# Second feed-forward of a hybrid block: where the pair stage keeps its activation sums and weight differences, and when the last adaLN rows are computed

## The chip, the cores and the metric

The kernel runs on one core of one Trainium2 chip. The metric is the device time of one execution in microseconds (us), the median of several runs. The engines are TensorE (PE, matmuls), VectorE (DVE), ScalarE (ACT), GpSimd (POOL) and SyncE (SP), whose queue issues nearly all DMAs here. Each engine works through its own instructions in a fixed order.

## The reference

One block with 256 rows of 2048 values, all in float32. A vector c gives, by a 2048 x 18432 matrix (adaLN), nine vectors of 2048: a shift, a scale and a gate for each of three parts. The parts are a feed-forward, a mixer (differential attention beside a convolution), and a second feed-forward:

```python
def swiglu(h, w_gu, w_down):
    gu = jnp.einsum('bsd,df->bsf', h, w_gu)
    g, u = jnp.split(gu, 2, axis=-1)
    return jnp.einsum('bsf,fd->bsd', jax.nn.silu(g) * u, w_down)
...
    h = modulate(rms_norm(x, ffn2_norm[l]), sh2, sc2)
    x = x + FFN_RESIDUAL_WEIGHT * g2[:, None, :] * swiglu(h, ffn2_w_gu[l], ffn2_w_down[l])
```

Here w_gu is 2048 x 11264 and w_down 5632 x 2048. The change touches the second feed-forward alone.

## The kernel before

**Products.** A float32 operand is split into two parts: hi, rounded to the fp32r type by a cast on ACT, and lo, the rest, by a subtraction on DVE. A product is three matmuls (mm3, L342, L346, L347): hi by hi, hi by the weight's lo, and lo by the weight's hi. A weight tile is 128 x 2048 values (1 MB), loaded into one of four raw buffers (L307) and split in two halves of 1024 columns (L318 on ACT, L320 on DVE) into four whi and four wlo buffers. A tile gives 24 matmuls of 512 columns: four row blocks by two row tiles (t) by three.

**adaLN.** The matrix is laid out as 144 rows of 128 x 2048 (ada, L195 and L196): each is loaded into a raw buffer too, and multiplied and summed with c, broadcast in the buffer c_bc, in one DVE instruction. Rows 96 to 127 are the scales and shifts of the second feed-forward, rows 128 to 143 its gates. ada_share(r, limit) adds r rows to a credit for each weight tile and computes a row when the credit reaches one; ada_until(j) computes all rows up to j at once.

**The second feed-forward** (ffn with base 96). Gate and up columns are taken in 22 chunks of 512 (256 of each). Chunks 0 to 13 go in the usual way: four weight tiles each, of which the first (k blocks 0 to 3) is done early, and its result kept in parts[c]. The norm comes in four pieces of 512 columns by two row tiles (Norm.piece): a DMA transposes it (turn), and complete scales and splits it; after_tiles(n, ...) puts a step off by n weight tiles. Chunks 14 to 21 go as four **pairs**: the two chunks' first tiles (b11, b21 in one raw buffer, b12, b22 in the other) are taken together in seven products in place of eight (pair_first, Winograd's form of Strassen), each of six matmuls. For that, pair_sums makes four sums of activations once for all pairs, and each pair makes four differences of weights. Six ordinary weight tiles complete a pair. Chunk 13 comes last, and then the product with w_down (down_strassen).

In pair_first the products stand in this order: b11 (into c22), b12 - b11 (c12), t2 = b22 - b12 (c22), b21 - t2 (c21), b21 (c11), t2 - b11 (c22), b22 (c12). Between them kept() copies c22 or c12 into a tmp buffer (L719), since c22 and c12 add up over several products.

finish(c, ...) turns a chunk's result into operands of w_down: it adds the kept part (L935), applies silu (L936) and the product (L937), a DMA transposes it, and a cast and a subtraction split it (L364, L365) into a block that lives until the end. It is called during the following chunk or pair.

**Buffers and order.** General blocks (blk, 28 of 4 KB a partition) hold the norm's operands (8), parts, finished chunks and whatever is in hand; tmp has 6 buffers. A scheduler sets each engine's order at build time, and a buffer goes to the next that asks when it comes free. Before, the sums of the pairs are put into c_bc (L680), so that all adaLN rows have to be done first: ada_until(144) stands ahead of pair_sums (L994).

## Time and profile before

| | |
|---|---|
| median of 3 runs | 1827.68 us (1826.13 to 1827.97) |
| the profiled execution | 1827.56 us, its span 1824.5 us |
| granted TensorE clock, mean | 0.995 |
| busy in the span | PE 98%, DVE 85%, ACT 58%; SP's DMA queue 75.7% of the 16 DMA engines' time |
| matmuls | 8009 |
| second feed-forward's pairs | four, from 1398.8 us to about 1568 us |

Times in the trace are counted from the start of the span. A matmul's duration (about 390 ns) overlaps with the next one's; what counts is the distance between starts. In the rows of a timeline stand the start, the duration, the engine, the line, the operation and the tiles; "x2" merges two in a row, and brackets give the idle time before and what ended it. A row by stretch has its bounds, its length, the busy time and (x) the instructions of PE, PEld (weight loads), DVE, ACT and POOL, then the granted clock, the share of the DMA engines and GB/s.

### The profile page before, as it was taken

Reading aid. Unit: us, or ns where it says so; the run is one execution under the profiler, and the core shown is the slowest. Engines: PE = TensorE matmul, PEld = TensorE weight load, DVE = VectorE, ACT = ScalarE, POOL = GpSimd, SP = SyncE. Lnnn points to the kernel's source line nnn. Section 1 sums busy time; section 2 is a strip of 40 time slices with the busy share of each in tenths; the row PEclk is TensorE's granted clock in tenths of the full one; section 3 lists DMA queues with packets and bytes.
Section 4 is the critical chain, followed back from the end, with each engine's and each line's share of the span. In section 5 each row is a group of like instructions: output and inputs, shape, how many; then the busy total and the mean of one; then the engine's idle time right before and its main releaser. Section 6 shows DMA issues by size and latency. Waiting matters only on the chain.

```text
span 1824.5 us, 21716 instructions
## 1 busy us (share of the span) xinstructions
PE 1790.1 (98%) x8009; PEld 1471.6 (81%) x8009; DVE 1551.4 (85%) x2000; ACT 1063.1 (58%) x1577; POOL 29.2 (2%) x29
## 2 busy tenths in 40 slices
PE   7999999999999999999999999999998999999998
PEld 5778888888888888888888888878887888878887
DVE  7889889898898778898999798797988777699877
ACT  7554455565454434567798647656665666555453
POOL 0000000000000000000110000000000000000000
PEclk8999999999999999999999999999999999999999
DMA  9979999898999888765444497898996666655552
GB/s 378 360 306 315 351 340 318 321 340 330 341 351 357 323 345 325 288 252 193 177 149 162 164 361 289 322 343 287 341 346 236 206 220 237 218 190 213 202 216 106
DMA packets 118138, 507.17 MB, mean 278 GB/s; under 512 B 53601, under 2 KB 54033, under 8 KB 60561
## 3 DMA queue, kind: packets, MB, share of 16 engines
q1 hardware_dynamic: 118032, 505.81, 75.7%
q8 instruction: 62, 1.02, 0.2%
q14 instruction: 44, 0.35, 0.1%
HBM read 492.37 MB, written 2.12 MB: 271 GB/s over the span
## 4 chain that ended last, share of the span: by engine, by line
PE 87%; DVE 8%; ACT 2%; issue 2%; DMA 1%; POOLq 0%; POOL 0%; DVEq 0%; SPq 0%; ACTq 0%
PE acc L346 27%; PE acc L347 27%; PE acc L342 26%; DVE wlo L320 2%; PE tp L342 2%; PE tp L347 2%; PE tp L346 2%; DVE raw L196 1%; DMA xall<-in_x_dram 1%; PE acc L1269 1%; ACT whi L318 1%; DVE blk L1161 1%; DVE wlo L551 0%; DVE blk L320 0%; ACT whi L550 0%
## 5 line engine op out<-in xcount | busy, mean ns | idle before, releaser
L346 PE MATMUL acc<-wlo,blk 128*128 128x512 f32 x2248 | 878.8, 391 | 10.0 <-DVE wlo L320 9.9
L342 PE MATMUL acc<-whi,blk 128*128 128x512 f32 x2251 | 873.6, 392 | 7.1 <-ACT whi L318 5.5
L347 PE MATMUL acc<-whi,blk 128*128 128x512 f32 x2248 | 877.0, 390 | 0.1
L318 ACT CAST whi<-raw 128x1024 fp32r<-128x1024 f32 x565 | 578.9, 1044 | 393.3 <-PE acc L347 246.2
L320 DVE TENSOR_TENSOR wlo<-raw,whi 128x1024 fp32r<-128x1024 f32 x565 | 669.4, 1209 | 152.2 <-ACT whi L318 151.1
L346 PEld LDWEIGHTS acc<-wlo,blk 128*128 128x128 f32 x2248 | 422.8, 188 | 105.0 <-DVE wlo L320 16.5
L342 PEld LDWEIGHTS acc<-whi,blk 128*128 128x128 f32 x2251 | 423.3, 188 | 96.0 <-ACT whi L318 6.8
L347 PEld LDWEIGHTS acc<-whi,blk 128*128 128x128 f32 x2248 | 422.7, 188 | 88.4 <-DVE blk L419 0.8
L196 DVE CUSTOM_DVE_ANT_0 raw<-raw,c_bc 128x2048 f32<-128x2048 f32 x142 | 323.9, 2283 | 1.1 <-DMA raw<-in_w_ada_dram 1.0
L550 ACT CAST whi<-raw 128x1024 fp32r<-128x1024 f32 (+1 forms) x56 | 52.9, 946 | 69.0 <-PE tp L347 31.9
L551 DVE TENSOR_TENSOR wlo<-raw,whi 128x1024 fp32r<-128x1024 f32 (+1 forms) x56 | 60.8, 1087 | 20.2 <-ACT whi L550 20.0
L936 ACT ACTIVATE blk<-blk 128x256 f32<-128x256 f32 x88 | 35.3, 416 | 64.1 <-DVE blk L935 63.9
L1161 DVE SCALAR_TENSOR_TENSOR blk<-blk,cst,blk 128x247 f32<-128x247 f32 (+21 forms) x176 | 70.3, 457 | 0.0
L770 ACT COPY blk<-acc 128x512 f32<-128x512 f32 x56 | 32.5, 589 | 44.0 <-PE acc L347 42.2
L935 DVE TENSOR_TENSOR blk<-acc,blk 128x512 f32<-128x512 f32 x72 | 47.2, 683 | 10.8 <-PE acc L347 10.8
L956 ACT COPY blk<-blk 128x1024 uint16<-128x1024 uint16 x33 | 44.2, 1355 | 9.6 <-DMA blk<-blk 9.5
L342 PE MATMUL tp<-whi,blk 128*128 128x512 f32 x127 | 49.4, 389 | 0.0
L346 PE MATMUL tp<-wlo,blk 128*128 128x512 f32 x127 | 49.4, 389 | 0.0
L347 PE MATMUL tp<-whi,blk 128*128 128x512 f32 x127 | 49.4, 389 | 0.0
L342 PE MATMUL acc<-blk,blk 128*128 128x512 f32 x104 | 40.7, 394 | 0.5 <-ACT blk L334 0.5
L346 PE MATMUL acc<-blk,blk 128*128 128x512 f32 x100 | 39.1, 391 | 0.5 <-DVE blk L320 0.5
L940 ACT COPY blk<-tmp 128x1024 uint16<-128x1024 uint16 x33 | 34.2, 1048 | 9.0 <-DVE tmp L937 8.7
(264 smaller groups left out, 1246.9 us busy)
## 6 DMA issues: line engine op xcount, KB each, us to landing
raw<-in_w_gu_dram SPq DMA_DIRECT2D x161, 1024.0 KB, 6.7
raw<-in_w_ada_dram SPq DMA_DIRECT2D x142, 1024.0 KB, 6.3
raw<-in_w_dn_dram SPq DMA_DIRECT2D x88, 1024.0 KB, 5.1
raw<-in_w_in_dram SPq DMA_DIRECT2D x40, 1024.0 KB, 4.8
raw<-in_w_out_dram SPq DMA_DIRECT2D x16, 1024.0 KB, 4.8
raw<-in_w_gu_dram SPq DMA_DIRECT2D x8, 768.0 KB, 5.7
blk<-in_w_gu_dram SPq DMA_DIRECT2D x10, 512.0 KB, 13.5
blk<-gate_line SPq DMA_DIRECT2D x6, 512.0 KB, 5.7
```

The source lines that it names most:

```text
L196: nc.vector.tensor_tensor_reduce(out=raw, in0=raw, in1=c_bc, scale=1.0, scalar=0.0, op0=ALU.mult, op1=ALU.add, accum_out=ada_cols[g][:, j ...
L318: nc.scalar.copy(out=hi[:, :m, :], in_=rw)
L320: nc.vector.tensor_sub(out=lo[:, :m, :], in0=rw, in1=hi[:, :m, :].bitcast(F32))
L342: nc.tensor.matmul(acc, ah, wh, start=start, stop=False, skip_group_check=more)
L346: nc.tensor.matmul(acc, ah, wl, start=False, stop=False, skip_group_check=more)
L347: return nc.tensor.matmul(acc, al, wh, start=False, stop=stop, skip_group_check=more)
L550: nc.scalar.copy(out=hi[:, :n, :], in_=src)
L551: nc.vector.tensor_sub(out=lo[:, :n, :], in0=src, in1=hi[:, :n, :].bitcast(F32))
L935: nc.vector.tensor_add(out=p[:, t, :], in0=accs[t], in1=us[t] if us else p[:, t, :])
L936: nc.scalar.activation(out=p[:, t, :256], in_=p[:, t, :256], func=AF.Silu)
L956: nc.scalar.copy(out=src.bitcast(U16).rearrange("p i t (s b) -> p b t i s", b=2), in_=turned.rearrange("p (b t i s) -> p b t i s", b=2, t= ...
L1161: nc.vector.scalar_tensor_tensor(out=y[:, d:], in0=u, scalar=w, in1=y[:, d:], op0=ALU.mult, op1=ALU.add)
```

## The change

Five things change, all in the second feed-forward:

- pair_sums puts its sums into two general blocks, which are in hand until the last pair's products; c_bc stays as it is until down_strassen.
- pair_first has no block t2. The differences are made in place, one after the other in b12 and b11, each as soon as the product of the one before is split.
- ada_until(144) goes. The rows go on in the pairs: credit for two tiles behind pair_first, and for one behind each of the six tiles.
- The rate of the rows in the single chunks and the pairs is 0.4 a tile in place of 0.72.
- In Norm.piece the steps of the second row tile of pieces 1 and 2 are put off by one weight tile more (behind = 2 + t).

```diff
-            behind = 1 if self.base == 0 or kb == 3 else 2
+            behind = 1 if self.base == 0 or kb == 3 else 2 + t
...
-        keep = cbp.tile([P, 2, 2, 4, P], F32R, tag="c_bc", name="sums")
+        keep_hi, keep_lo = blk([P, 2, 4, P], F32R), blk([P, 2, 4, P], F32R)
...
-            hi, lo = keep[:, 0, j], keep[:, 1, j]
+            hi, lo = keep_hi[:, j], keep_lo[:, j]
...
-        t2 = blk([P, 2, 512])
+        w11 = split(b11)
         nc.vector.tensor_sub(out=b12, in0=b12, in1=b11)
-        nc.vector.tensor_sub(out=t2, in0=b22, in1=b12)
-        times(c22, lambda j: act(j, 0), split(b11), True)
+        times(c22, lambda j: act(j, 0), w11, True)
         u11 = kept(c22)
-        nc.vector.tensor_sub(out=b11, in0=t2, in1=b11)
         times(c12, lambda j: sums[j][0], split(b12), True)
         u22 = kept(c12)
-        times(c22, lambda j: sums[j][1], split(t2))
+        nc.vector.tensor_sub(out=b12, in0=b22, in1=b12)
+        times(c22, lambda j: sums[j][1], split(b12))
         u12 = kept(c22)
-        nc.vector.tensor_sub(out=t2, in0=b21, in1=t2)
-        times(c21, lambda j: act(2 + j, 1), split(t2), True)
+        nc.vector.tensor_sub(out=b11, in0=b12, in1=b11)
+        nc.vector.tensor_sub(out=b12, in0=b21, in1=b12)
+        times(c21, lambda j: act(2 + j, 1), split(b12), True)
...
-                ada_until(144)
                 sums = pair_sums(st)
...
                 us = pair_first(w_gu, c, act, sums, banks)
+                ada_share(2 * ada_b[0], ada_b[1])
...
                         mm_tile(banks[2 * n:2 * n + 2], w, act, 4 * pc, False, pc == 3, more=True)
+                        ada_share(*ada_b)
...
-    ffn(norm2, w_gu2, w_dn2, 128, (0.72, 128), (0.72, 144), None, [], [[c] for c in range(3, 10)], [])
+    ffn(norm2, w_gu2, w_dn2, 128, (0.72, 128), (0.4, 144), None, [], [[c] for c in range(3, 10)], [])
```

The new lines of pair_first stand in the changed kernel at L728 (b22 - b12), L731 (into b11) and L732 (b21 - b12); L723 is the first difference in both.

First place, DVE, the last steps of the sums before the pairs. L196 is an adaLN row (its second entry reads the sum out), L683 to L689 form the sums, L692 splits them, L935 and L937 belong to the chunk before. Before:

```order
L196 ISA raw_11290,ada_10985<-raw_11290,c_bc 128x2048
L196 ISA ada_10985 128x1
L687 TENSOR_TENSOR tmp_11309<-tmp_11309,tmp_11307 128x128
L935 TENSOR_TENSOR blk_9647<-acc_11162,blk_9647 128x512
L196 ISA raw_11293,ada_10985<-raw_11293,c_bc 128x2048
L196 ISA ada_10985 128x1
L689 TENSOR_TENSOR tmp_11309<-tmp_11307,tmp_11309 128x128
L201 TENSOR_TENSOR ada_10985<-ada_10985,cst 128x8
L937 TENSOR_TENSOR tmp_11356<-blk_9647 128x256
L935 TENSOR_TENSOR blk_9647<-acc_11163,blk_9647 128x512
L692 TENSOR_TENSOR sums<-tmp_11300,sums 128x512
L692 TENSOR_TENSOR sums<-tmp_11309,sums 128x512
```

And now, from the first step of the sums on:

```order
L683 TENSOR_TENSOR tmp_11282<-blk_9035,blk_9036 128x512
L689 TENSOR_TENSOR tmp_11275<-tmp_11273,tmp_11275 128x128
L686 TENSOR_TENSOR tmp_11284<-tmp_11282 128x128
L688 TENSOR_TENSOR tmp_11284<-tmp_11282 128x128
L687 TENSOR_TENSOR tmp_11284<-tmp_11284,tmp_11282 128x128
L320 TENSOR_TENSOR wlo_11297<-raw_11293,whi_11295 128x1024
L692 TENSOR_TENSOR blk_11272<-tmp_11275,blk_11271 128x512
L689 TENSOR_TENSOR tmp_11284<-tmp_11282,tmp_11284 128x128
L365 TENSOR_TENSOR blk_11328<-blk_9605,blk_11328 128x512
L196 ISA raw_11374,ada_11373<-raw_11374,c_bc 128x2048
L196 ISA ada_11373 128x1
L692 TENSOR_TENSOR blk_11272<-tmp_11284,blk_11271 128x512
```

Two of the last three rows stand above among the steps of the second sum, the third just ahead of them; now the steps follow each other, with one row ahead of the last split.

Second place, DVE in the second pair, up to the low half of the fourth operand. L710 is the low half of an operand of the pair, named by what it is split from; L935 belongs to the pair before. Before:

```order
L724 TENSOR_TENSOR blk_11753<-raw_11751 128x1024
L320 TENSOR_TENSOR wlo_11719<-raw_11711,whi_11717 128x1024
L710 TENSOR_TENSOR wlo_11757<-raw_11749,whi_11756 128x1024
L935 TENSOR_TENSOR blk_11836<-acc_11433,tmp_11454 128x512
L727 TENSOR_TENSOR raw_11749<-blk_11753,raw_11749 128x1024
L710 TENSOR_TENSOR wlo_11770<-raw_11751,whi_11769 128x1024
L935 TENSOR_TENSOR blk_11836<-acc_11434,tmp_11512 128x512
L710 TENSOR_TENSOR wlo_11782<-blk_11753,whi_11781 128x1024
L935 TENSOR_TENSOR blk_11845<-acc_11435,tmp_11479 128x512
L732 TENSOR_TENSOR blk_11753<-raw_11749,blk_11753 128x1024
L935 TENSOR_TENSOR blk_11845<-acc_11436,tmp_11467 128x512
L710 TENSOR_TENSOR wlo_11795<-blk_11753,whi_11794 128x1024
```

And now:

```order
L935 TENSOR_TENSOR blk_11825<-acc_11412,tmp_11431 128x512
L710 TENSOR_TENSOR wlo_11754<-raw_11738,whi_11753 128x1024
L196 ISA raw_11822,ada_11373<-raw_11822,c_bc 128x2048
L196 ISA ada_11373 128x1
L728 TENSOR_TENSOR raw_11738<-raw_11738 128x1024
L935 TENSOR_TENSOR blk_11825<-acc_11413,tmp_11490 128x512
L731 TENSOR_TENSOR raw_11736<-raw_11738,raw_11736 128x1024
L710 TENSOR_TENSOR wlo_11767<-raw_11738,whi_11766 128x1024
L935 TENSOR_TENSOR blk_11834<-acc_11414,tmp_11456 128x512
L732 TENSOR_TENSOR raw_11738<-raw_11736,raw_11738 128x1024
L935 TENSOR_TENSOR blk_11834<-acc_11415,tmp_11443 128x512
L710 TENSOR_TENSOR wlo_11781<-raw_11738,whi_11780 128x1024
```

L724, which makes the third operand in a block of its own ahead of all splits, is gone; L728 makes it behind the low half of the second operand, and an adaLN row stands between the two.

ACT in the same pair: L709 is the cast of an operand, L719 the copy of a product. Before, from the third operand on:

```order
L709 CAST whi_11781<-blk_11753 128x1024
L936 ACTIVATE blk_11836<-blk_11836 128x256
L936 ACTIVATE blk_11845<-blk_11845 128x256
L719 COPY tmp_11766<-tp_11748 128x512
L709 CAST whi_11794<-blk_11753 128x1024
L719 COPY tmp_11779<-tp_11747 128x512
L709 CAST whi_11804<-raw_11749 128x1024
L719 COPY tmp_11791<-tp_11748 128x512
L709 CAST whi_11814<-raw_11749 128x1024
```

And now:

```order
L709 CAST whi_11766<-raw_11738 128x1024
L936 ACTIVATE blk_11825<-blk_11825 128x256
L719 COPY tmp_11751<-tp_11735 128x512
L719 COPY tmp_11763<-tp_11734 128x512
L936 ACTIVATE blk_11834<-blk_11834 128x256
L719 COPY tmp_11776<-tp_11735 128x512
L709 CAST whi_11780<-raw_11738 128x1024
L709 CAST whi_11790<-raw_11736 128x1024
L709 CAST whi_11800<-raw_11736 128x1024
```

The cast of the fourth operand stood behind the first copy, and stands now behind the third.

Third place, ACT in the fourth pair, from the fifth operand on; L318 casts the tile behind the pair, L364 splits finished chunks. Before:

```order
L709 CAST whi_12450<-raw_12395 128x1024
L719 COPY tmp_12425<-tp_12393 128x512
L709 CAST whi_12460<-raw_12395 128x1024
L719 COPY tmp_12437<-tp_12394 128x512
L709 CAST whi_12472<-raw_12397 128x1024
L936 ACTIVATE blk_12491<-blk_12491 128x256
L318 CAST whi_12502<-raw_12500 128x1024
L936 ACTIVATE blk_12491<-blk_12491 128x256
L318 CAST whi_12506<-raw_12500 128x1024
L719 COPY tmp_12470<-tp_12394 128x512
```

And now:

```order
L709 CAST whi_12447<-raw_12393 128x1024
L709 CAST whi_12457<-raw_12393 128x1024
L709 CAST whi_12469<-raw_12395 128x1024
L318 CAST whi_12499<-raw_12497 128x1024
L364 CAST blk_12280<-blk_12157 128x512
L364 CAST blk_12284<-blk_12166 128x512
L318 CAST whi_12503<-raw_12497 128x1024
L318 CAST whi_12533<-raw_12531 128x1024
L719 COPY tmp_12433<-tp_12392 128x512
```

The third copy (tmp_12437, now tmp_12433) stood behind the cast of the sixth operand, and stands now behind three casts of later tiles and two splits of chunks of the second pair.

## The prediction

> **What bounds the kernel now.** I read the page first, then the waits of TensorE (PE), then busy time by stretch, then the timeline at the one place that stands out.
>
> ```profile
> PE 1790.1 (98%) x8009; PEld 1471.6 (81%) x8009; DVE 1551.4 (85%) x2000; ACT 1063.1 (58%) x1577; POOL 29.2 (2%) x29
> PE acc L342 <- ACT whi L318: 4.6, 1, 4.6
> 1350.00:1400.00 50.00, 45.02 (x184) 35.90 (x183) 43.88 (x56) 25.43 (x30) 0.00 (x0) 0.93 0.81 294
> 1400.00:1450.00 50.00, 50.00 (x220) 40.61 (x219) 38.22 (x38) 32.84 (x41) 0.00 (x0) 1.00 0.54 176
> 1450.00:1500.00 50.00, 50.00 (x221) 41.02 (x220) 38.98 (x42) 34.16 (x41) 0.00 (x0) 1.00 0.68 223
> 1500.00:1550.00 50.00, 50.00 (x221) 41.12 (x220) 37.09 (x38) 33.55 (x41) 0.00 (x0) 1.00 0.69 248
> ```
>
> PE is busy 98% of the span, and the change neither adds nor takes a matmul: it can only remove or add PE waits. The second row is the longest wait behind the first 15 us, 4.6 us. It lies in the stretch 1350 to 1400 (184 matmuls where the next stretches have 220 and 221, granted clock 0.93), just before the four pairs. The pairs themselves (1400 to 1550) run without a wait, with 11 to 13 us of every 50 free on VectorE (DVE).
>
> ```profile
> 1373.78 0.39 PE L346 MATMUL acc<-wlo,blk 128*128 128x512 f32 x1
> 1374.00 0.39 PE L347 MATMUL acc<-whi,blk 128*128 128x512 f32 x1
> 1379.04 1.22 PE L342 MATMUL acc<-whi,blk 128*128 128x512 f32 x2 [4.64 <-ACT whi L318]
> ...
> 1385.33 0.52 PE L346 MATMUL acc<-wlo,blk 128*128 128x512 f32 x1
> 1385.69 0.40 PE L347 MATMUL acc<-whi,blk 128*128 128x512 f32 x1
> 1382.00:1384.00 2.00, 2.00 (x6) 1.57 (x5) 2.00 (x2) 1.08 (x2) 0.00 (x0) 0.50 0.24 98
> 1386.00:1388.00 2.00, 2.00 (x11) 1.64 (x10) 1.23 (x1) 0.24 (x1) 0.00 (x0) 1.00 0.73 303
> ```
>
> Matmuls follow each other by 0.227 us at full clock. From 1374.00 to 1385.69 only 15 start, worth 3.4 us, so this place costs 11.7 - 3.4 = **8.3 us**: 4.6 of waiting, and the rest because the clock then stands at 0.50 until 1385.5.
>
> **The change, part by part.** *The gap goes.* The cast PE waits for stands on ScalarE (ACT) behind the casts of the sums (L691), and those wait for a DVE chain between whose steps three adaLN rows stand (the order of before, in the section on the change). With the rows spread, the sums' steps stand in the changed order together, about three tiles ahead of the first pair. DVE does then, in the last 16.3 us before the pairs, six halves of weights (6.8), the sums (about 4), one row (2.2) and some 2.5 of other steps: 15.5 of 16.3, and it runs four halves (10.9 us) ahead. I see no new wait there: -8.3.
>
> *Norm pieces.* Behind = 2 + t delays only the completion of the second row tile of pieces 1 and 2 by one weight tile.
>
> ```profile
> 1193.39 2.28 DVE L196 CUSTOM_DVE_ANT_0 raw<-raw,c_bc 128x2048 f32<-128x2048 f32 x1
> ...
> 1196.34 1.37 DVE L890 TENSOR_TENSOR blk<-acc,blk 128x512 f32<-128x512 f32 x2
> 1197.63 2.35 DVE L320 TENSOR_TENSOR wlo<-raw,whi 128x1024 fp32r<-128x1024 f32 x2
> 1198.89 0.50 PE L346 MATMUL acc<-wlo,blk 128*128 128x512 f32 x1 [1.46 <-DVE wlo L320]
> 1197.00:1199.00 2.00, 0.54 (x3) 0.12 (x2) 2.00 (x4) 1.97 (x4) 0.00 (x0) 1.00 0.83 348
> ```
>
> PE waits here 1.46 us for the half that DVE splits at 1197.63, behind two L890 steps. In the changed order one of the two stands behind that half, so it starts some 0.7 earlier: -0.8 (between 0 and the whole 1.5).
>
> *The differences in place, and the rows beside them.* I call the seven products of a pair p1 to p7, their split operands #1 to #7, and the start of p1 zero. A product is six matmuls, 1.36 us. The second pair of before:
>
> ```profile
> L342 PE MATMUL tp<-whi,sums x16: 389/389/497, 1442.7 to 1535.3; 128*128 128x512 f32 x16
> 1436.10 1.05 ACT L709 CAST whi<-raw 128x1024 fp32r<-128x1024 f32 x1 [1.71 <-PE acc L347]
> 1442.86 0.59 ACT L719 COPY tmp<-tp 128x512 f32<-128x512 f32 x1 [0.67 <-PE tp L347]
> 1443.34 1.05 ACT L709 CAST whi<-blk 128x1024 fp32r<-128x1024 f32 x1
> 1444.42 1.23 DVE L710 TENSOR_TENSOR wlo<-blk,whi 128x1024 fp32r<-128x1024 f32 x1 [0.95 <-ACT whi L709]
> 1478.02 0.68 DVE L935 TENSOR_TENSOR blk<-acc,tmp 128x512 f32<-128x512 f32 x1
> 1478.62 1.22 DVE L727 TENSOR_TENSOR raw<-blk,raw 128x1024 f32<-128x1024 f32 x1
> 1479.75 1.22 DVE L710 TENSOR_TENSOR wlo<-raw,whi 128x1024 fp32r<-128x1024 f32 x1
> 1371.56 2.28 DVE L196 CUSTOM_DVE_ANT_0 raw<-raw,c_bc 128x2048 f32<-128x2048 f32 x1
> 1373.77 0.08 DVE L196 DVE_READ_ACCUMULATOR2_ANT ada<- 128x1 f32 x1
> ```
>
> p2 starts at 1442.7, so zero is 1442.7 - 1.36 = 1441.3. The cast of #4 starts at 1443.34, behind the copy of p1 (L719), and its low half is ready at 1444.42 + 1.23 = 1445.65, that is 4.3; p4 starts at 3 x 1.36 = 4.1 and uses the low half in its second matmul, at 4.3. So #4 comes just in time: **whatever delays it, PE pays in full.** On DVE a step of 1024 costs 1.13 from start to start (1478.62 to 1479.75), L935 0.60, an adaLN row 2.21.
>
> Before, #3 is computed (L724) ahead of the pair into its own block. Now it overwrites b12, so it has to follow the split of #2, whose cast waits until PE frees a buffer: it ends at 1437.15, that is -4.2. From there the changed order on DVE gives: low half of #2 to -3.0, adaLN row to -0.8, L728 to 0.3, L935 to 0.9, L731 to 2.1, low half of #3 to 3.2, L935 to 3.8, L732 to 5.0. p3's second matmul, due at 2.95, starts at 3.2, and p3 ends at 4.4. ACT now copies p3 ahead of the cast of #4: copy to 5.1, cast to 6.2, low half to 7.4. p4's second matmul starts at 7.4 instead of 4.3: **+3.1**. The later operands follow by 1.13 each, faster than a product, and add nothing.
>
> The same steps for the other pairs. First: the row stands ahead of #2 (row to -3.7, #2 to -2.5, L365, L728, L731, #3 to 1.6, L935, L732 to 3.4), the copy of p3 behind the cast; low half of #4 at 5.8: +1.5. Third: as the second, with two small steps more: +3.4. Fourth: no row, and the same walk brings #4 at 4.4, so in place costs nothing by itself.
>
> But the fourth pair has another wait. The sums hold two of 28 blocks, where before one (t2) was taken and given back in each pair. With 8 blocks of activations, 13 finished chunks, one part, two chunks of the first pair, two sums and two of the second in hand, all 28 are taken; the second pair's chunks can't be split (L364, L365) until p5 frees the first activations. Behind that stand the sums of the third pair (L935), and behind those the copy of p3, which lacks a tmp buffer.
>
> ```profile
> 1417.51 0.62 ACT L364 CAST blk<-blk 128x512 fp32r<-128x512 f32 x1
> 1418.17 0.69 DVE L365 TENSOR_TENSOR blk<-blk,blk 128x512 fp32r<-128x512 f32 x1 [1.56 <-ACT blk L364]
> 1406.26 2.00 ACT L318 CAST whi<-raw 128x1024 fp32r<-128x1024 f32 x2
> ```
>
> p5 ends at 7.1. ACT does two L364 (to 8.7), two casts L318, the second only when p7 has freed its buffer (9.6 to 10.7), and then the copy (11.3). DVE does #7 (8.2), two L365 (9.5) and the four L935 (12.0), the first of which frees the tmp buffer in time; then the low half of the first tile behind the pair (13.1). So p6 starts at 11.3, and that tile goes on at 13.2, with the 47th matmul since zero, due at 46 x 0.227 = 10.4: **+2.8**. It is 0.5 if the blocks come free in time (what #7 costs alone), and 4 if each step slips by a few tenths.
>
> *The queue of SyncE.* Seven rows' loads move among the weights and take one of four raw buffers each.
>
> ```profile
> raw<-in_w_gu_dram SPq DMA_DIRECT2D x161, 1024.0 KB, 6.7
> raw<-in_w_ada_dram SPq DMA_DIRECT2D x142, 1024.0 KB, 6.3
> ```
>
> The second weight of a pair (b12, b22) now goes out when the row ahead of it is done on DVE, about -14.3; with 6.7 to land it is there at -7.6, L723 is done at -6.4, #1 at -5.3, and #2 isn't late. The row inside the pair goes out at -13.2, needed at -3.0: covered by 4. Were the cover gone, DVE would stand in order behind the row, a microsecond for a microsecond.
>
> The sum, against the profiled execution (1827.56, span 1824.5, 0.12 below the median of the runs): -8.3 - 0.8 + 1.5 + 3.1 + 3.4 + 2.8 = +1.7, that is **1829.3 us**.
>
> **The rivals.** *The clock falls again (slower).* In pairs 2 and 3 PE waits 1.8 us, starts one matmul, and waits 1.0 more. At 1.46 us the clock stayed at 1.00 (the row of 1197), at 4.64 it fell; nothing between is shown. If one matmul doesn't count, the two waits are one of 2.8. A fall costs 8.3 - 4.6 - 0.2 (a second wait there) = 3.4: two make 1836. It decides if the clock looks at a share of busy time. The Trainium skill (TensorE: Matmul & The Clock Gate, Why this matters for your kernels) asks for no idle gaps over about 3 us between bursts. By that, these waits leave the clock alone and the sum stays 1829.3; the two rows of this trace agree with it.
>
> *The rows find room (faster).* If a row's step comes earlier than the buffer for #2, it costs nothing: DVE has 11 to 13 us free in 50, and the walk takes every step in order at its latest. If the waits of the pairs come to 3 in place of 10.8: 1821.5. Against it: pairs of before are just in time with no row.
>
> *Rows land late (slower).* If three of the seven rows come 1.5 us late: 1833.8. For it: loads of 1024 KB take 6.3 to 6.7. Against it: the cover above.
>
> *The gap stays.* If it was made by late weights and not by the rows, 8.3 come back: 1837.6. Against it: the wait names a cast, and ACT had the sums' casts ahead of it.
>
> **How the numbers follow.** This kernel's measurement tells about 0.2% (3.7 us) from no change. Forecast, 1829.3 (its own range 1826.5 to 1831.2, the pairs' waits 8 to 12.7): 0.52, and it is within 0.2%. Rows find room, 1821.5: 0.17, faster. Clock 0.16, late rows 0.10, gap stays 0.05: slower, 0.31 together. The range runs from 1821.5 to 1836.0; it leaves out half of the faster case and, above, the last one and some of the clock's.
>
> **What would show it.** Right: no 4.6 us wait before the pairs and a clock of 1.00 there; PE waits of 2 to 3 us in each of pairs 2 and 3, before p4, put down to ACT L709 or DVE L710; one of about 2 us in pair 4, before p6, put down to the copy of p3. A clock under 1.00 between the pairs speaks for the first rival, PE without waits there for the second, DVE waits for a load of w_ada in the pairs for the third. Pairs' waits under 5 or over 14 us in all make the forecast wrong.

## The result, and the profile after

The changed kernel takes 1836.3 us, the median of six runs (1833.5 to 1843.2), against 1827.8 before (1826.1 to 1828.4): a ratio of 1.0052, 95% interval 1.0035 to 1.0070. That is 8.5 us slower, where the prediction had 1829.3 and a range that ended at 1836.0. The profiled execution is the fastest of the six: 1833.5 us, span 1831.4, that is 6.9 longer than before.

The gap before the pairs is gone, as forecast. By stretch, the same 12 us of the kernel before and of the changed one:

```profile
1374.00:1386.00 12.00, 7.13 (x18) 4.88 (x17) 10.24 (x16) 7.41 (x10) 0.00 (x0) 0.72 0.84 265
```

```profile
1374.00:1386.00 12.00, 12.00 (x54) 9.95 (x53) 11.02 (x16) 5.90 (x7) 0.00 (x0) 1.00 0.87 289
```

PE runs 54 matmuls there in place of 18, at a clock of 1.00. But the pairs, which had no wait at all before, now have these, the four longest entries of PE's waits from 1390 to 1550 (the total in us, how often, the longest):

```profile
PE acc L342 <- ACT whi L709: 5.5, 5, 1.6
PE acc L346 <- DVE wlo L710: 1.8, 3, 0.8
PE tp L342 <- ACT whi L318: 1.1, 1, 1.1
PE tp L342 <- ACT tmp L719: 0.7, 1, 0.7
```

The second pair on PE, with the names p1 to p7 and #1 to #7 of the prediction, from p3's first matmul to p4's first; the last row is p5's first matmul, which now runs ahead of p4's second:

```profile
1439.20 0.39 PE L342 MATMUL tp<-whi,blk 128*128 128x512 f32 x1
1439.87 0.50 PE L346 MATMUL tp<-wlo,blk 128*128 128x512 f32 x1 [0.28 <-DVE wlo L710]
...
1440.90 0.40 PE L347 MATMUL tp<-whi,blk 128*128 128x512 f32 x1
1442.92 0.51 PE L342 MATMUL acc<-whi,blk 128*128 128x512 f32 x1 [1.62 <-ACT whi L709]
1443.87 0.50 PE L342 MATMUL acc<-whi,blk 128*128 128x512 f32 x1 [0.44 <-ACT whi L709]
```

Matmuls follow by 0.227 when nothing is late. Whatever two starts are further apart than that is lost: here 0.44 at p3's second matmul, 1.79 ahead of p4 (1442.92 - 1440.90 - 0.23), 0.72 behind p4's first: 2.95. The cause stands on DVE as the prediction walked it:

```profile
1432.37 1.23 DVE L710 TENSOR_TENSOR wlo<-raw,whi 128x1024 fp32r<-128x1024 f32 x1 [0.94 <-ACT whi L709]
1433.51 2.29 DVE L196 CUSTOM_DVE_ANT_0 raw<-raw,c_bc 128x2048 f32<-128x2048 f32 x1
1435.72 0.08 DVE L196 DVE_READ_ACCUMULATOR2_ANT ada<- 128x1 f32 x1
1435.72 1.22 DVE L728 TENSOR_TENSOR raw<-raw 128x1024 f32<-128x1024 f32 x1
...
1440.33 1.22 DVE L732 TENSOR_TENSOR raw<-raw,raw 128x1024 f32<-128x1024 f32 x1
1441.46 0.69 DVE L935 TENSOR_TENSOR blk<-acc,tmp 128x512 f32<-128x512 f32 x1
1442.90 1.22 DVE L710 TENSOR_TENSOR wlo<-raw,whi 128x1024 fp32r<-128x1024 f32 x1 [0.75 <-ACT whi L709]
```

The low half of #2, the adaLN row, L728, then the chain to L732, and the low half of #4 at 1442.90: DVE waits for nothing from 1432.37 on but once, for the cast of #4.

Summed in this way over every place, in us, each from the one profiled execution of the kernel; the median beside it is that of all its executions. A star is one window of half clock (3.41 us, worth about 1.7; the section on the hardware), included in the number:

| kernel | ahead of the pairs, 1255 to 1386 | pair 1 | pair 2 | pair 3 | pair 4 | median | ratio to before, 95% interval |
|---|---|---|---|---|---|---|---|
| before | 8.6 ** | 0.2 | 0.1 | 0.2 | 0.1 | 1827.8 | |
| changed, profiled | 0.8 | 3.7 | 3.2 | 5.6 * | 3.3 | 1836.3 | 1.0035 to 1.0070 |
| 1: rate 0.82 alone | 6.2 | 0.3 | 0.1 | 0.2 | 0.1 | 1825.5 | 0.9982 to 0.9999 |
| 2: and in place | 5.6 | 4.2 * | 0.8 | 0.8 | 0.8 | 1829.6 | 1.0007 to 1.0025 |
| 3: sums in blocks, not in place | 0.6 | 8.7 ** | 0.2 | 0.1 | 0.6 | 1829.3 | 1.0005 to 1.0023 |
| 4: both, rows ahead | 0.8 | 9.7 ** | 0.8 | 0.8 | 3.3 | 1835.4 | 1.0031 to 1.0058 |
| 5: rows late in the pairs | 0.2 | 6.8 ** | 5.4 * | 5.7 * | 3.4 | 1840.0 | 1.0059 to 1.0086 |
| 6: changed, again | 3.9 * | 3.3 | 4.8 * | 5.6 * | 3.3 | 1837.5 | 1.0046 to 1.0071 |
| 7: norm pieces alone | 9.2 ** | 0.2 | 0.2 | 0.1 | 0.1 | 1826.8 | 0.9992 to 1.0009 |
| 8: two rows earlier | 4.5 | 0.2 | 0.1 | 0.2 | 0.1 | 1823.6 | 0.9974 to 0.9992 |
| 9: other differences in place | 6.1 | 1.6 | 3.7 * | 2.1 | 2.1 | 1831.9 | 1.0017 to 1.0037 |
| 10: cast ahead of copy | 0.3 | 6.0 * | 4.8 * | 6.1 * | 3.4 | 1838.4 | 1.0040 to 1.0065 |
| 11: three rows earlier, 0.66 | 5.2 | 0.2 | 0.2 | 0.2 | 0.1 | 1824.0 | 0.9979 to 0.9996 |
| 12: no row in pair 1 | 0.0 | 5.6 * | 6.0 * | 2.7 | 3.4 | 1837.5 | 1.0051 to 1.0078 |
| 13: copy behind the cast in pair 1 | 0.0 | 5.9 ** | 3.2 | 5.6 * | 3.3 | 1835.8 | 1.0032 to 1.0062 |
| 14: both of these | 1.9 | 2.0 | 6.3 ** | 2.7 | 3.4 | 1833.9 | 1.0025 to 1.0053 |

Changed against before, in the two profiles: -7.8 ahead of the pairs, and +3.5, +3.1, +5.4 and +3.2 in the pairs, +7.4 together, for 6.9 more of span; most of the rest was gained in the first 40 us, where the two kernels are alike.

### The profile page after: what moved, and what is told of

It reads as the page before. It is cut to its first block, busy times and chain, and to the rows that moved or that the text cites. A ratio compares the mean times of both kernels' runs of the same rounds, so it can differ in the third digit from the quotient of the medians.

```text
span 1831.4 us, 21722 instructions
## 1 busy us (share of the span) xinstructions
PE 1791.6 (98%) x8009; PEld 1470.7 (80%) x8009; DVE 1552.3 (85%) x2000; ACT 1065.6 (58%) x1577; POOL 29.2 (2%) x29
## 5 line engine op out<-in xcount | busy, mean ns | idle before, releaser
L318 ACT CAST whi<-raw 128x1024 fp32r<-128x1024 f32 x565 | 579.3, 1044 | 397.7 <-PE acc L347 241.1
L320 DVE TENSOR_TENSOR wlo<-raw,whi 128x1024 fp32r<-128x1024 f32 x565 | 670.0, 1211 | 150.6 <-ACT whi L318 149.2
L196 DVE CUSTOM_DVE_ANT_0 raw<-raw,c_bc 128x2048 f32<-128x2048 f32 x142 | 324.1, 2285 | 4.1 <-DMA raw<-in_w_ada_dram 4.1
L342 PE MATMUL tp<-whi,blk 128*128 128x512 f32 x143 | 56.0, 391 | 1.8 <-ACT whi L318 1.1
L956 ACT COPY blk<-blk 128x1024 uint16<-128x1024 uint16 x33 | 44.4, 1355 | 21.3 <-DMA blk<-blk 21.3
L346 PE MATMUL tp<-wlo,blk 128*128 128x512 f32 x143 | 55.9, 391 | 0.3 <-DVE wlo L710 0.3
L347 PE MATMUL tp<-whi,blk 128*128 128x512 f32 x143 | 55.7, 389 | 0.0
L935 DVE TENSOR_TENSOR blk<-acc,blk 128x512 f32<-128x512 f32 x72 | 47.1, 684 | 9.9 <-PE acc L347 9.9
L709 ACT CAST whi<-raw 128x1024 fp32r<-128x1024 f32 x28 | 28.4, 1050 | 26.4 <-PE acc L347 10.0
L710 DVE TENSOR_TENSOR wlo<-raw,whi 128x1024 fp32r<-128x1024 f32 x28 | 33.4, 1222 | 10.9 <-ACT whi L709 10.8
L342 PE MATMUL acc<-blk,blk 128*128 128x512 f32 x104 | 40.7, 394 | 0.7 <-ACT blk L334 0.7
```

The source lines that it names most:

```text
L196: nc.vector.tensor_tensor_reduce(out=raw, in0=raw, in1=c_bc, scale=1.0, scalar=0.0, op0=ALU.mult, op1=ALU.add, accum_out=ada_cols[g][:, j ...
L318: nc.scalar.copy(out=hi[:, :m, :], in_=rw)
L320: nc.vector.tensor_sub(out=lo[:, :m, :], in0=rw, in1=hi[:, :m, :].bitcast(F32))
L342: nc.tensor.matmul(acc, ah, wh, start=start, stop=False, skip_group_check=more)
L346: nc.tensor.matmul(acc, ah, wl, start=False, stop=False, skip_group_check=more)
L347: return nc.tensor.matmul(acc, al, wh, start=False, stop=stop, skip_group_check=more)
```

## The experiments

Each kernel is the kernel before or the changed one with the edit shown. Losses are those of the table.

**1. The burst of rows alone.** The kernel before, rate 0.82.

```diff
-    ffn(norm2, w_gu2, w_dn2, 128, (0.72, 128), (0.72, 144), None, [], ...)
+    ffn(norm2, w_gu2, w_dn2, 128, (0.72, 128), (0.82, 144), None, [], ...)
```

> Of the change nothing is kept but the idea that no burst of adaLN rows stands ahead of the sums: the kernel before with the rate of the rows at 0.82 a tile in place of 0.72, so that all 16 are done when the sums are made (sums in c_bc, third difference in its own block, no row in the pairs). Theory (the burst of rows among the sums' steps made the gap of 8.3 us before the pairs, and nothing else in the change gains): about 1819.5, no wait before the pairs, pairs without a wait as before. Rival (the gap comes from late weights or from the sums themselves): it stays, about 1827.8.

Measured 1825.5, 1.4 faster than the runs of before beside it. The wait of 4.6 and the fall of the clock are gone, so the burst did make the gap. But the faster rate brought waits of its own, 6.2 us of them. PE's waits from 1326 to 1356 and, in the second fence, from 1356 to 1381:

```profile
1332.38 0.50 PE L346 MATMUL acc<-wlo,blk 128*128 128x512 f32 x1 [1.46 <-DVE wlo L320]
1355.35 0.50 PE L346 MATMUL acc<-wlo,blk 128*128 128x512 f32 x1 [0.53 <-DVE wlo L320]
```

```profile
1362.54 0.50 PE L346 MATMUL acc<-wlo,blk 128*128 128x512 f32 x1 [1.46 <-DVE wlo L320]
1380.48 0.50 PE L346 MATMUL acc<-wlo,blk 128*128 128x512 f32 x1 [0.97 <-DVE wlo L320]
```

**2. And the differences in place.** As 1, with the pair_first of the changed kernel (L720 to L733), sums in c_bc.

> The first experiment's kernel (rate 0.82, sums in c_bc) with the differences made in place. No adaLN row stands in a pair. Theory (the in-place chain alone is just in time, as the walk gives low half #4 at 4.3 without the row, and it is the row of 2.2 us inside it that PE pays for): PE waits of at most 0.5 us a pair, about 1819.5 to 1821. Rival (the chain in place is itself too long, row or no row): some 3 us in each of pairs 1 to 3, about 1828.5.

Measured 1829.6: 4.1 more than the first. Both were partly wrong. Pairs 2 to 4 lose 0.8 each with no row inside, neither nothing nor 3: of the 3.2 and the 3.9 (without half clock) that pairs 2 and 3 lose in the changed kernel, the chain in place is 0.8. Pair 1 loses 2.5 besides half clock, with no row near: there the low half of #2 starts 3.3 us ahead of p1, in pair 2 4.1, and two short steps more (L365 and an L935) stand between it and the last difference.

**3. The sums in blocks, differences not in place.**

```diff
     (of the changed kernel:)
-    (0.4, 144)
+    (0.72, 144)
...
+        t2 = cbp.tile([P, 2, 512], F32, tag="c_bc", name=nm("t2"))
         nc.vector.tensor_sub(out=b12, in0=b12, in1=b11)
+        nc.vector.tensor_sub(out=t2, in0=b22, in1=b12)
     (and on as in the kernel before)
```

> The sums in two general blocks, as in the changed kernel, but the third difference in a place of its own as in the kernel before (it takes c_bc, which is free, because all rows are done ahead of the pairs: rate 0.72 with the credit of the three tiles behind the sums). Theory (the wait of pair 4, 2.9 us in the changed kernel, comes from the shortage of general blocks alone): pair 4 still waits before p6 or at the first tile behind, 2 to 4 us in all, pairs 1 to 3 have no waits; about 1822.5. Rival (that wait comes from the differences in place): pair 4 without a wait, about 1819.5.

Measured 1829.3. Pair 4 loses 0.6: the blocks alone don't make its wait. Pair 1 loses 8.7, which neither theory had: with credit from the tiles behind the sums, rows run at 1375.7 and 1382.0, and the cast of the first operand waits for its weights (ACT, this kernel):

```profile
1388.58 1.05 ACT L709 CAST whi<-raw 128x1024 fp32r<-128x1024 f32 x1 [1.34 <-DMA raw<-in_w_gu_dram]
```

This pair's two loads go out at 1383.4 and 1384.1, in the changed kernel at 1374.3 and 1376.1. The second is released by the row of 1382.0, which had the raw buffer. The first stands in SyncE's queue right behind a transposing DMA, and that the rows delayed it too isn't shown.

**4. The changed kernel with all rows ahead.**

```diff
-    (0.4, 144)
+    (0.72, 144)
```

> The changed kernel with the rate back at 0.72 a tile, so that all 16 rows are done before the first pair and none stands inside one; sums in general blocks and differences in place as changed. Theory (rows in the chain cost pairs 1 to 3 some 10 us, blocks cost pair 4 some 3): waits of pairs 1 to 3 at most 0.5 each, pair 4 as in the changed kernel; about 1822.5. Rival (the chain in place alone): pairs 1 to 3 keep their waits of about 3 us each, about 1832.

Measured 1835.4, above the rival's time (1832) and far from the theory's (1822.5); yet the places speak against the rival. Pairs 2 and 3 fall to 0.8 each, as in the second experiment, so there it was the row. Pair 4 has the same 3.3 as the changed kernel; with the second and third experiments (0.8 and 0.6), blocks and in place together make it, neither by itself. The largest loss is in pair 1, 9.7, where the weights come late as in the third (the first operand's cast waits 1.25 for them).

**5. The rows in the pairs, but late in them.**

```diff
-                ada_share(2 * ada_b[0], ada_b[1])
...
-                        ada_share(*ada_b)
+                        if pc > 1:
+                            ada_share(2 * ada_b[0], ada_b[1])
```

> The changed kernel, with the rows that run beside the pairs put elsewhere: no credit behind pair_first and behind the pair's first two tiles, double credit behind the four tiles after them. As many rows in the pairs, sums in blocks and differences in place, but on DVE no row stands between the pair's second and third operand. Theory (it is the place of the row in the chain that costs, not that rows run beside the pairs): waits of pairs 1 to 3 fall from 10.3 us to under 2, pair 4 as in the changed kernel, about 1823 to 1825. Rival (rows beside the pairs cost wherever they stand, by their loads or by DVE's time): pairs 1 to 3 keep 8 us or more, about 1833 or over.

Measured 1840.0, the slowest of all. The rival has the time, but the reason isn't shown to be its reason. In pair 2 the row ends at 1431.15, and DVE then waits twice for casts (0.87 and 1.25), so that it isn't the row that holds the chain; two steps L935 now stand ahead of the first difference (1434.38 to 1435.58) and another ahead of L728. Moving a row rearranged the steps around it; what rows cost outside the chain stays open.

**6. The changed kernel again.**

> The changed kernel once more, unaltered, to see whether the scatter of its times (1833.5 to 1843.2, where the kernel before has 1826.1 to 1828.4) goes with the granted clock. Theory (the waits in pairs 1 to 3 are near the point at which the clock falls, so that it falls in some executions in more places than in others): times differ by 2 us or more, the longer ones with the lower mean clock (about 0.001 of clock for 2 us), and stretches of pairs with a clock under 1.00 in the profile. Rival (loads of rows land late in some executions): the clock is the same and the waits themselves are longer, named as waits for a load.

Five times from 1834.4 to 1839.9, median 1837.5. The profiled one, 1838.0, has a span of 1836.2, 4.8 longer than the first profile of the same kernel. The table shows where: the waits of pairs 2 to 4 are the same to a few hundredths, those of pair 1 come to 3.1 in place of 3.5, but pair 2 has a window of half clock (1.7), and the wait that was 0.55 at 1336 is 2.22 and brings another (3.1 together):

```profile
1338.32 0.80 PE L346 MATMUL acc<-wlo,blk 128*128 128x512 f32 x1 [2.22 <-DVE wlo L320]
```

So both theories hold a part: the clock, and loads, since ACT's waits for weights between 1230 and 1390 rose from 2.3 to 6.4 us. The mean clock of a run doesn't rank the times (1839.9 at 0.997, 1838.0 at 0.994), as it holds the start of the kernel too. Why one execution's loads land later isn't known.

**7. The norm pieces alone.** The kernel before with the first edit of the change.

```diff
-            behind = 1 if self.base == 0 or kb == 3 else 2
+            behind = 1 if self.base == 0 or kb == 3 else 2 + t
```

> The kernel before with the change in the norm pieces alone (behind = 2 + t). Theory (the wait of 1.5 us at 1197 only moves to a half that is split some tiles later, as in the changed kernel, where 0.95 and 1.63 us are lost in place of 1.62 and 0.95): no change, within 0.5 us of the kernel before. Rival (the forecast's term): 0.8 us faster, between 0 and 1.5.

Measured 1826.8, ratio 1.0001: no change. The waits of 1.46 and 0.79 that the kernel before has at 1198.9 and 1210.8 have only moved to other halves. PE's waits from 1196 to 1208 in this kernel:

```profile
1196.99 0.73 PE L342 MATMUL acc<-whi,blk 128*128 128x512 f32 x2 [0.42 <-ACT whi L318]
1198.25 0.50 PE L346 MATMUL acc<-wlo,blk 128*128 128x512 f32 x1 [0.52 <-DVE wlo L320]
1205.46 0.50 PE L346 MATMUL acc<-wlo,blk 128*128 128x512 f32 x1 [1.46 <-DVE wlo L320]
```

The changed kernel has 0.79 at 1197.9 and 1.47 at 1205.1.

**8. Two rows earlier.** The kernel before, rows to 130 in the stage of first weight tiles.

```diff
-    (0.72, 128), (0.72, 144)
+    (0.72, 130), (0.72, 144)
```

> The kernel before with one number changed: rows of the stage of first weight tiles may go on to row 130 in place of 128, so that two gate rows are done between 1237 and 1260 us, where the kernel before does none (there DVE is busy 13.5 of 20 us and the DMA engines 0.70), and no burst is left ahead of the sums. Theory (the first experiment won little because the DMA engines and DVE are full from 1260 to 1370 us, so that its faster rate made waits of 6.2 us there; room, not the number of rows, decides): the gap of 8.3 goes and nothing comes instead, about 1819.5. Rival (any 16 rows ahead of the sums cost some 6 us somewhere): about 1825.5, as in the first experiment.

Measured 1823.6, ratio 0.9983 (0.9974 to 0.9992): 3.4 us faster than before, and the fastest kernel here. The gap is gone, but 4.5 us stand between 1286 and 1368 in other waits, though the rate there is that of the kernel before. Stretch 1260 to 1360, before and this kernel:

```profile
1260.00:1360.00 100.00, 100.00 (x443) 82.78 (x442) 92.06 (x109) 70.58 (x86) 0.00 (x0) 1.00 1.00 343
```

```profile
1260.00:1360.00 100.00, 96.96 (x424) 78.94 (x423) 90.45 (x109) 68.36 (x83) 0.00 (x0) 1.00 0.99 334
```

DVE and the DMA engines do nearly the same work in both, and only one of them makes PE wait. So "room decides" fell. What is left is the order, which row meets which step; no run changes that alone, so it is argued and not shown.

**9. Other differences in place.** As 2, the sixth operand made ahead.

```diff
-        nc.vector.tensor_sub(out=b12, in0=b12, in1=b11)
+        nc.vector.tensor_sub(out=b11, in0=b12, in1=b11)
+        nc.vector.tensor_sub(out=b12, in0=b22, in1=b12)
...
-        nc.vector.tensor_sub(out=b12, in0=b22, in1=b12)
-        times(c22, lambda j: sums[j][1], split(b12))
+        nc.vector.tensor_sub(out=b11, in0=b22, in1=b11)
+        times(c22, lambda j: sums[j][1], split(b11))
...
-        nc.vector.tensor_sub(out=b11, in0=b12, in1=b11)
-        nc.vector.tensor_sub(out=b12, in0=b21, in1=b12)
-        times(c21, lambda j: act(2 + j, 1), split(b12), True)
+        nc.vector.tensor_sub(out=b11, in0=b21, in1=b11)
+        times(c21, lambda j: act(2 + j, 1), split(b11), True)
...
-        times(c22, lambda j: sums[j][2], split(b11))
+        times(c22, lambda j: sums[j][2], split(b12))
```

> The second experiment's kernel (rate 0.82, sums in c_bc, no row in a pair, differences in place), with the differences taken so that one step less lies between the second operand's split and the fourth operand: b12 - b11 overwrites b11, b22 - b12 (which is the sixth operand) overwrites b12 at once, and then b22 - b11 and b21 - b11 follow in b11. Theory (the wait of 0.78 us a pair in the second experiment, and 2.7 in its first pair, is the length of the chain in place: two differences and two splits one behind the other, with the sixth operand's step of 1.13 among them): the waits of pairs 2 to 4 fall to 0.2 or less and that of pair 1 by about 1.1; 1826 to 1827. Rival (the waits come from the reuse of the raw buffers, or from the order of the copies on ACT, whatever the chain's length): 1829.6 as in the second experiment.

Measured 1831.9, 2.2 slower than the second. Pair 1 fell by 1.0, as the theory had it; pairs 2 to 4 rose to 2.1. The chain didn't get shorter there: the freed place was taken by two steps of the pair before. DVE in pair 3 of this kernel:

```profile
1484.95 1.23 DVE L729 TENSOR_TENSOR raw<-raw,raw 128x1024 f32<-128x1024 f32 x1
1486.09 1.28 DVE L935 TENSOR_TENSOR blk<-tp,tmp 128x512 f32<-128x512 f32 x2
1487.37 1.22 DVE L710 TENSOR_TENSOR wlo<-raw,whi 128x1024 fp32r<-128x1024 f32 x1
1488.63 1.22 DVE L732 TENSOR_TENSOR raw<-raw 128x1024 f32<-128x1024 f32 x1
```

**10. The cast of #4 ahead of the copy of p3.** The changed kernel.

```diff
+            cast[0] = nc.scalar.copy(out=hi, in_=src)      (in split)
...
-        u12 = kept(c22)
...
+        w4 = split(b12)
+        with tc.issue_after(cast[0].ins):
+            u12 = kept(c22)
+        times(c21, lambda j: act(2 + j, 1), w4, True)
```

> The changed kernel with one order fixed on ACT: the copy of the third product has to stand behind the cast of the fourth operand (in the changed kernel it stands ahead of it in pairs 2 and 3). Theory (DVE's chain sets the time: in pair 2 the last difference ends at 1441.5 and the third product at about 1441.3, so that the copy of 0.5 us delays the cast by 0.3 to 0.5 alone): the wait of 1.62 in pairs 2 and 3 falls by 0.3 to 0.5 each, about 1 us in all; 1835 to 1836.5, less where the shorter waits keep the clock from falling. Rival (the place of the copy on ACT is the cause and the row on DVE is not): waits of pairs 2 and 3 fall to 0.78 each as in the second experiment, 1831 or less.

Measured 1838.4, within the scatter of the changed kernel. The rival fell. The theory's size was too large as well: in pair 2 p4's first matmul gains 0.2 and the one behind it loses 0.3. The place of this copy on ACT costs nothing that shows; DVE's chain sets the time.

**11. Three rows earlier, then fewer.** The kernel before.

```diff
-    (0.72, 128), (0.72, 144)
+    (0.72, 131), (0.66, 144)
```

> The kernel before with rows allowed to 131 in the stage of first weight tiles and a rate of 0.66 behind it (3 rows early, 13 in the 20 tiles, none left ahead of the sums). Theory (room decides: at 0.66 a tile, 1260 to 1370 us holds fewer rows than in the kernel before, which has no wait there): the waits of 4.1 us that the eighth experiment still had between 1286 and 1345 fall below 1; about 1819.5 to 1820.5. Rival (which tile a row meets decides, not their number): waits of 3 to 4 us remain at other places, 1823.5.

Measured 1824.0: the rival's. With fewer rows a tile, 5.2 us of waits stand ahead of the pairs, at 1265, 1287, 1299 and 1334, where the kernel before has none.

**12. No row in pair 1.** The changed kernel.

```diff
-                ada_share(2 * ada_b[0], ada_b[1])
+                if i:
+                    ada_share(2 * ada_b[0], ada_b[1])
```

> The changed kernel without the credit behind the first pair's products: no row stands inside the first pair's chain; in pair 2 one stands there as before, and in pairs 2 and 3 one stands directly ahead of the low half of the fourth operand. Theory (a row costs by how much it delays the low half of the fourth operand): pair 1 falls from 3.7 us to about 2.7, what the chain in place costs there without a row (second experiment: 4.2 with 1.5 of half clock); pairs 2 and 3 lose 1 to 1.5 us for the row ahead of the low half, beside 3.2 and 0.8; total about that of the changed kernel, 1835 to 1838. Rival (pair 1 is late because a copy on ACT, L956, waits for a DMA ahead of the cast of the second operand, whatever DVE does): pair 1 keeps 3.7.

Measured 1837.5. Pair 1 keeps its waits: the four of them come to 3.8, in the changed kernel to 3.5, as the rival said. With no row, DVE stands idle 3.3 us for the cast of the second operand:

```profile
1388.80 1.23 DVE L710 TENSOR_TENSOR wlo<-raw,whi 128x1024 fp32r<-128x1024 f32 x1 [3.30 <-ACT whi L709]
```

Of the theory, what it said of pair 1 failed (2.7). On pairs 2 and 3 it was right in kind: a row directly ahead of the low half of #4 costs 1.4 in pair 2 (waits of 4.4, in the changed kernel 3.0) and 1.9 in pair 3 (2.7 against 0.8 with no row in the fourth experiment), the second more than the 1 to 1.5 forecast.

**13. The copy L956 behind the cast, pair 1.** The changed kernel, where ACT holds the second operand's cast like this:

```profile
1382.58 1.06 ACT L709 CAST whi<-raw 128x1024 fp32r<-128x1024 f32 x1 [1.54 <-PE acc L347]
1386.70 1.36 ACT L956 COPY blk<-blk 128x1024 uint16<-128x1024 uint16 x1 [3.06 <-DMA blk<-blk]
1387.93 1.04 ACT L709 CAST whi<-raw 128x1024 fp32r<-128x1024 f32 x1
```

On DVE the row is done at 1387.99, and the low half of #2 then waits 0.93 more for that cast:

```profile
1385.77 2.29 DVE L196 CUSTOM_DVE_ANT_0 raw<-raw,c_bc 128x2048 f32<-128x2048 f32 x1
1387.99 0.08 DVE L196 DVE_READ_ACCUMULATOR2_ANT ada<- 128x1 f32 x1
1389.01 1.23 DVE L710 TENSOR_TENSOR wlo<-raw,whi 128x1024 fp32r<-128x1024 f32 x1 [0.93 <-ACT whi L709]
```

```diff
+                with tc.issue_after(second[0].ins) if len(second) == 1 else nullcontext():
-                nc.scalar.copy(out=src.bitcast(U16)...
+                    nc.scalar.copy(out=src.bitcast(U16)...
...
+        w12 = split(b12)
+        second.append(cast[0])
```

> The changed kernel with two instructions of ACT exchanged in the first pair: the copy L956 of a chunk ahead, which waits 3 us for its transposing DMA, has to stand behind the cast of the second operand; all else stands as in the changed kernel, the row too. Theory (in the first pair the cast of the second operand is held by that copy, 1387.9 in place of about 1386.3, when the buffer comes free; behind it DVE still has the row to 1388.0): the low half of the second operand starts about 1.0 earlier and the chain 0.8 to 1.0 earlier, pair 1 loses about 2.7 in place of 3.5; about 1 us less than the changed kernel, 1835.5. Rival (the row alone holds the chain): no change, pair 1 at 3.5 and 1836.5.

Measured 1835.8, too near 1836.3 to tell apart. The waits of pair 1 come to 3.0 where they came to 3.5 (0.8 less was expected), but to 3.1 in the sixth experiment, which has the copy, so that these sums alone show no gain. The steps show what holds the chain: with the cast early, the low half of #2 starts without a wait, when the row ends, at 1389.15.

**14. Copy behind, and no row, in pair 1.** Experiments 12 and 13 together.

> The twelfth experiment's kernel (no row in the first pair's chain) with the same exchange on ACT in the first pair. Theory (row and copy each hold the second operand's split till about the same time, so that taking one away alone gains little and both together more): the low half of the second operand starts at about 1387.4, 1.4 earlier than in the twelfth experiment, and pair 1's waits fall from 3.8 (without half clock) to about 2 or less. Rival (the first pair's wait is the chain in place itself, with whatever stands ahead of it): it stays at 2.7 or more, as in the second experiment.

Measured 1833.9, and the waits of pair 1 come to 1.9, as expected (PE, this kernel):

```profile
1398.16 0.50 PE L342 MATMUL acc<-whi,blk 128*128 128x512 f32 x1 [0.67 <-ACT whi L711]
1399.43 0.49 PE L346 MATMUL acc<-wlo,blk 128*128 128x512 f32 x1 [0.76 <-DVE wlo L712]
```

With both 3.5 (3.1 in the sixth experiment, 4.2 in the tenth), without the row 3.8, without the copy 3.0, without either 1.9. The two run beside each other, and taking one away leaves the other.

One number joins five of these profiles. In the changed kernel, its second profile and experiments 10, 12 and 13 the steps from the low half of #2 to the cast of #4 are the same, and the cast starts 7.12 to 7.13 us behind that low half. So the waits of pair 1 are 5.03 us plus the start of the low half of #2, counted from p1's start:

| | start of #2's low half | waits of pair 1 |
|---|---|---|
| changed, profiled | -1.53 | 3.5 |
| 6: changed, again | -1.97 | 3.1 |
| 10: cast ahead of copy | -0.82 | 4.2 |
| 12: no row in pair 1 | -1.20 | 3.8 |
| 13: copy behind the cast | -2.03 | 3.0 |

Whatever delays that half is paid in full, and with neither row nor copy it starts at -4.0. There the sum would give 1.0 and not 1.9, because two steps change places and one of them waits 0.60 for a cast (L364).

## Why the prediction was wrong

Its sum was +1.7 and the profile has +6.9; the median has +8.5. Step by step:

- *The gap goes: -8.3.* Right: the 8.3 of before are gone. The stretch was forecast as free; a wait of 0.55 came at 1336, behind a row and steps of a chunk, which in another execution was 2.2 with half clock behind it. Ahead of the pairs the profile has -7.8.
- *Norm pieces: -0.8.* Wrong: 0.0. The wait moved to a later half, as the seventh experiment shows with nothing else changed. The step looked at one half and not at the one into whose way the L890 steps came.
- *Pair 1: +1.5.* **This step failed**: 3.5. From the low half of #2 on the walk was right: it had that half start at -3.7, and the sum found in experiment 14 then gives 5.03 - 3.7 = 1.3. But the half starts at -1.53, 2.2 later. The walk had only the row ahead of it, to -3.7. The row ends at -2.55. With the row behind #1, as it stands in the trace, the walk's own figures (#1 at -5.3, 2.2 for a row) already give -3.1. Another 1.0 goes to the cast of #2, which the walk put at the time its buffer came free. On ACT stood a copy that waits 3.06 us for a transposing DMA. Experiments 12 to 14 show that copy and row hold the chain side by side. Even without both, 1.9 is left.
- *Pair 2: +3.1.* Right: 3.1 more than before, by the steps of the walk.
- *Pair 3: +3.4.* 3.7 more than before, besides half clock. Right in kind, the row and the chain; the fourth experiment takes the row out and leaves 0.8 in each of the two.
- *Pair 4: +2.8.* 3.2. The forecast's places are there: PE waits for the cast of a tile behind the pair (1.14) and for the copy of p3 (0.68). Its reason was too simple: blocks alone (third) give 0.6, in place alone (second) 0.8, both 3.3.
- *"In place costs nothing by itself."* Wrong by 0.7 a pair, and by 2.3 in pair 1; 4.1 us between the medians of experiments 1 and 2. It is inside the pairs' numbers above, not beside them.
- *The clock.* **The sum had this at nothing, and that failed too.** The first rival, with 0.16, came true in part: the first profile has one window of half clock, the second (1838.0) three, some 5 us. That the clock is what carries the median past the range is likely and not shown, since no other execution was profiled. The prediction weighed whether a wait of 1.8 and one of 1.0 count as one, and priced a fall at 3.4 (its own terms, 8.3 - 4.6 - 0.2, give 3.5). That was the price of the 6.8 us of half clock in the kernel before, two windows; one window costs 1.7 and doesn't come in every execution: none in pair 2 of the first profile, one in that of the sixth experiment. The rule taken from the Trainium skill (TensorE: Matmul & The Clock Gate, Why this matters for your kernels), no idle gaps of over about 3 us, isn't strict enough here: in pair 3 waits of 1.62 and 0.45 with a matmul between them brought half clock.

So the mechanism of the pairs was forecast and mostly its size; the sum failed by pair 1 (+2.0), the clock (+1.7 in the profiled execution, more in others), the norm (+0.8), the stretch ahead of the pairs (+0.5) and pairs 3 and 4 (+0.3 and +0.4): 5.7 together, 5.2 by the span.

## What to carry to other kernels

Where the trace shows an operand that is just in time, walk both engines that make it, and on each everything that stands ahead in its order, with what that waits for: here the second cast was late for a copy that had nothing to do with the pair. When two things hold a chain side by side, taking one away shows nothing; take both. And count a gap's removal as gained only when the work that made it has been given another place: the same 16 rows, spread in three ways ahead of the pairs, left 4.5 to 6.2 us of waits there, in place of 8.6 (experiments 1, 8 and 11).

## What the runs showed of the hardware

The clock is set by windows of 3.41 us on a fixed grid. In all 16 profiles the trace's record of the clock changes only at whole multiples of 3.413 us from each other, and a window at half clock follows one in which PE had little to do. Pair 3 of the changed kernel, one row a window:

```profile
1486.73:1490.14 3.41, 1.40 (x5) 0.59 (x4) 2.17 (x4) 2.89 (x5) 0.00 (x0) 1.00 0.00 0
1490.14:1493.55 3.41, 3.35 (x8) 2.74 (x9) 3.41 (x4) 2.29 (x4) 0.00 (x0) 0.50 0.00 0
1493.55:1496.97 3.42, 3.42 (x17) 2.81 (x16) 3.04 (x7) 2.74 (x4) 0.00 (x0) 1.00 0.88 323
```

Five matmuls fall into the first window, the next runs at 0.50, the one behind it at 1.00 again. At full clock a window holds 15, at half 7.5, so that 7.5 x 0.227 = 1.7 us are lost. Pair 2 of the same execution, its waits lying across a border of the grid:

```profile
1438.94:1442.35 3.41, 2.08 (x8) 1.05 (x6) 3.21 (x4) 2.02 (x4) 0.00 (x0) 1.00 0.28 118
1442.35:1445.77 3.42, 2.41 (x9) 1.72 (x10) 2.87 (x3) 3.42 (x5) 0.00 (x0) 1.00 0.00 0
```

And pair 2 in the sixth experiment, the same kernel with the same waits, which fall into one window:

```profile
1444.03:1447.44 3.41, 1.35 (x6) 0.46 (x4) 2.64 (x4) 2.93 (x5) 0.00 (x0) 1.00 0.00 0
1447.44:1450.85 3.41, 3.41 (x9) 2.73 (x9) 3.30 (x3) 2.73 (x4) 0.00 (x0) 0.50 0.18 22
```

In these rows nothing but the place on the grid tells the two apart. I counted the time without a matmul (each worth 0.227) in every window from 1100 to 1815 us of the 16 profiles. The 22 windows at full clock with a half one behind them have 2.02 to 3.41 us free; of more than 3,000 followed by full clock only four have 2.0 or more, the largest 2.20. So for these matmuls the point lies between 2.0 and 2.2 us free of 3.41, in one wait or in several. The Trainium skill (TensorE: Matmul & The Clock Gate, Part 1: The HAM clock gate) has the free-running window of 3413 ns, and these traces agree; that the clock falls after an idle window they narrow to one that is some 60% idle.

With waits near that point, the same kernel can differ from one execution to the next by 1.7 us for a pair, as pair 2 did in the two profiles. That is likely a part of why the changed kernel's six runs lie 9.7 us apart, where the six of before lie 2.3 apart. Only two executions of the changed kernel were profiled, so how much of the rest is late loads, as in the sixth experiment, stays open.
